# An encoder block in fp32r triples: the squares of x by rows, with ScalarE's accumulator in place of GpSimd's adds

## The chip, the cores and the metric

One core of a Trainium2 chip runs the whole program. The metric is the device time of one execution in microseconds (us), as the median of several runs. The kernel before took 2014.98 us (three runs, 2014.74 to 2017.5).

## The reference, cut to what matters

The input x has 512 rows (tokens) of 2048 columns, all float32. One transformer layer with two attention mixers is computed:

```
h    = rmsnorm(x, g_mix)                      # x * rsqrt(mean(x*x, over 2048 columns) + 1e-6) * g_mix
proj = h @ w_in                               # 2048 x 4608: qA, kA, vA, qB, kB, vB
...                                           # mixer A (grouped queries, axial rotary), mixer B (dilated windows)
x = x + concat(rmsnorm(A), rmsnorm(B)) @ w_out
x = x + (silu(h2 @ w_gate) * (h2 @ w_up)) @ w_down      # h2 = rmsnorm(x, g_ffn)
return rmsnorm(x, g_final)
```

The change is in the first line. The kernel multiplies x times the gain, without the norm, by w_in, and scales rows of the product afterwards by r = rsqrt(mean(x*x) + 1e-6). So the sum of squares of each row of x isn't needed before the first products are scaled.

## The kernel before, in words

**Products.** Every matrix product is made of three TensorE matmuls on fp32r numbers (mm3, L235 to L237): an operand is split into a rounded part "hi" and the rest "lo", and hi times hi, hi times lo and lo times hi are added up. A weight tile of 128x512 is split by a copy on ScalarE (hi; L287, or L776 in column blocks) and a subtraction on VectorE (lo; L292, or L779). So every weight that TensorE multiplies costs one 128x512 operation on each of these two engines.

**Units.** The program is a list of units, worked off in order by the loop at the end (L1309 ff.). A unit is one weight tile and its matmuls. Units 0 to 15 are the 16 chunks (128 of the 2048 columns of x) of the first projection block, keys and values of mixer A, "kvA" (first_chunk): 12 matmuls each, on all four row tiles of x. From unit 16 on stands the first "column block" (ColBlock), whose units have 6 matmuls each: it forms sums and differences of blocks, as Strassen's scheme does, and so needs sums of quarters of x (x_sums, L355) and their splits (x_split, L350 and L351), and sums of weight tiles (L816). Later come the second column block, the attention, the output projection and the feed-forward layer; they are not touched.

**What the loop does for unit n.** It issues the load of chunk n+5 of x (load_x, on SyncE's queue, SP). It prepares chunk n+1 (x_prep): four transposes on TensorE into a PSUM bank (L316), a copy of it with the gain on ScalarE (L330), hi on ScalarE (L331), lo on VectorE (L332), and row_squares, below. It then loads and splits weights some units ahead (prepare), issues the matmuls of unit n, what follows a unit (post), and what is hung on unit n (hook). For chunk pairs the hooks are, two and three units after the pair is there, x_sums (four VectorE operations of 128x256) and x_split (three operations on ScalarE, three on VectorE); and on GpSimd's queue a store of one form to DRAM (L336). Each engine works off its own instructions in the order in which the loop issued them, and starts none ahead of one that still waits.

**Squares, before.** row_squares(k) is issued within x_prep(k). ScalarE squares the chunk in place (L370; chunk 0 goes to sq1, L368), as a tile of 128 rows by 4 row tiles by 128 columns, and GpSimd adds the 128x512 squares to sq1 (L371), from chunk 1 on. The hook of unit 20 (make_r1) reduces sq1 over the columns on VectorE (L387) and makes r of it by a power on GpSimd (L217); the evictions of the column block (L864) wait for r.

**Homes.** Tiles of 128x512 numbers for loads are handed out from a list, "homes": at first 20 of the tile stage and 3 of the tile early (its fourth is sq1). A chunk of x takes one, which goes back behind its square and add; a weight takes one, which goes back when it is split, and goes to the next load in the list. The four of early leave the list at unit 12 (EARLY_HOMES; one that is in use then comes back later), and four of a tile "more" join it at unit 21. When unit 15 ends, post_plain evicts the four PSUM banks of kvA on ScalarE (L470), each into a home, from which a DMA on ScalarE's own queue stores it to DRAM (L457).

Of the kernel before, what the change touches and what calls it, by code (L numbers as in the profile page):

```python
# [11 lines left out]
F32 = mybir.dt.float32  # L12
# [44 lines left out]
HEAD_RATE = (1.42, 1.9)  # L57
TURN_LAG = 6
VALUE_LAG = 8
EARLY_HOMES = 12  # L60
COLUMN_BLOCKS = 2


# [5 lines left out]
def encoder_block(ctx, tc, x, g_mix, w_in, g_q_a, g_k_a, g_out_a, g_out_b, w_out, g_ffn,  # L69
# [40 lines left out]

    xs = [None] * KD
    stage = wp.tile([P, 20, 512], F32, tag="stage", bufs=1, name="stage")
    homes = deque(stage[:, n] for n in range(20))
    homing = [True]
    extra_homes, retired = {}, []

# [11 lines left out]
    def leave_homes():  # L128
        homing[0] = False
        homes.clear()  # L130

    def load_x(k):
        xs[k] = homes.popleft().rearrange("p (t c) -> p t c", t=NT)
        nc.sync.dma_start(xs[k], x[0, :, k * P:(k + 1) * P].rearrange("(t p) c -> p t c", p=P))

    fixed = cp.tile([P, 512], F32, name="fixed")
# [176 lines left out]
    def x_prep(k):  # L313
        ps = bank()
        for t in range(NT):
            nc.tensor.transpose(ps[:, t * P:(t + 1) * P], xs[k][:, t, :], ident)  # L316
        i, half = divmod(k, 2)
        if half == 0:
            xpair[i] = in_turn(pairs_turn, 3, [P, 4 * 512], F32, "xpair")
        flat = xpair[i][:, half * 1024:half * 1024 + 512]  # L320
        view = flat.rearrange("p (f c) -> p f c", c=256)
        hi, lo = (form_pair(3 * half, i, j) for j in range(2))
        gain = gm[:, k:k + 1]
        if k == 0:
            ps3 = ps.rearrange("p (f c) -> p f c", c=256)
            nc.scalar.activation(hi, ps3, AF.Copy, scale=gain)
            nc.vector.scalar_tensor_tensor(lo, ps3, gain, f32(hi), op0=OP.mult, op1=OP.subtract)
            nc.scalar.activation(flat, ps, AF.Copy, scale=gain)
        else:
            nc.scalar.activation(flat, ps, AF.Copy, scale=gain)  # L330
            nc.scalar.activation(hi, view, AF.Copy)  # L331
            nc.vector.tensor_tensor(lo, view, f32(hi), op=OP.subtract)  # L332
        release(ps)
        row_squares(k)
        if half == 0:
            hook(k, lambda: nc.gpsimd.dma_start(ar_dram[:, i], arena[0][:, 1, i]))  # L336
        else:
            hook(k + 2, lambda: x_sums(i))
            hook(k + 3, lambda: x_split(i))
# [18 lines left out]
        tt(s2, s1, a_l)  # L358
        tt(s4, b_l, s2)

    early = sp.tile([P, 4, 512], F32, tag="rowss", bufs=1, name="early")
    more_homes("early", early)
    sq1 = [homes.pop()]

    def row_squares(k):
        home = xs[k].rearrange("p t c -> p (t c)")
        if k == 0:
            nc.scalar.activation(sq1[0], home, AF.Square)  # L368
        else:
            nc.scalar.activation(home, home, AF.Square)  # L370
            nc.gpsimd.tensor_tensor(sq1[0], sq1[0], home, op=OP.add)  # L371
        homes.append(home)

    def col_sums(src):
        ps = bank()
# [8 lines left out]

    def make_r1():
        ss = small()
        nc.vector.tensor_reduce(ss, sq1[0].rearrange("p (t c) -> p t c", t=NT), axis=AX.X, op=OP.add)  # L387
        r1["r"] = rsqrt_mean(ss, NT, D)
        r1["rs"] = small()
        nc.vector.tensor_scalar(r1["rs"], r1["r"], HD ** -0.5, None, op0=OP.mult)  # L390
# [997 lines left out]
```

## Time and profile before

| | before |
|---|---|
| median of 3 runs | 2014.98 us |
| profiled execution, its own time | 2016.21 us |
| its span | 2014.4 us (27421 instructions) |
| granted TensorE clock, mean | 0.997 |
| TensorE (PE) busy | 1984.7 us (99%) |
| VectorE (DVE) busy | 1573.3 us (78%) |
| ScalarE (ACT) busy | 1113.9 us (55%) |
| GpSimd (POOL) busy | 154.0 us (8%) |

The profile is one execution. Times in it count from the start of the span; the execution's own time is 1.8 us longer than the span. A row of the timeline gives the start, the time, the engine, the line, the operation, the tile written and the tiles read, the shape, how many instructions alike follow each other, and in brackets how long the engine had been idle before and what ended that. A row of a group gives the busy time in us, the mean of one in ns, and the idle time in front of it. A row of the windows gives, for PE, PEld (weight loads of TensorE), DVE, ACT and POOL, busy us and the number of instructions in a stretch, then the granted clock, the share of the DMA engines and GB/s. Starts of one engine in succession lie closer than the times of single instructions, since these overlap by some 0.1 us.

### The profile page before, as it was taken

What the parts mean: (1) busy time and instruction counts of PE and PEld (TensorE: products, weight loads), DVE (VectorE), ACT (ScalarE), POOL (GpSimd) and SP (SyncE); (2) the same over time, 40 slices, a digit from 0 to 9 for tenths busy, and PEclk for the clock granted to TensorE, in tenths of its full rate; (3) what the DMA queues carried; (4) which work ended last, traced back from release to release, by engine and by line L of the source; (5) the groups of instructions that cost most, each with busy time, mean ns of one, the idle gap of its engine ahead of it and who ended that gap; (6) DMA issues with size and microseconds to landing.
All of it is one profiled execution on the core that took longest, in us unless ns stands there. A gap on an engine that the chain in (4) does not pass through costs nothing. (4 is left out here: it accounts for less than half of the span.)

```text
span 2014.4 us, 27421 instructions
## 1 busy us (share of the span) xinstructions
PE 1984.7 (99%) x9019; PEld 1630.5 (81%) x9019; DVE 1573.3 (78%) x2781; ACT 1113.9 (55%) x1972; POOL 154.0 (8%) x172
## 2 busy tenths in 40 slices
PE   8999999999999999999999999999999999999998
PEld 6788888887788888888888888888888887788886
DVE  7988866567754688878877878878779886977967
ACT  7655345556544565555555545455555665666656
POOL 4100100000010000000000000000000121111121
PEclk9999999999999999999999999999999999999999
DMA  8576533335244545737647657558468798779865
GB/s 268 188 262 223 184 116 104 110 115 184 89 137 150 200 138 201 272 120 261 239 137 273 203 182 274 170 189 285 146 215 269 194 248 257 188 175 274 207 146 165
DMA packets 231391, 390.61 MB, mean 194 GB/s; under 512 B 21408, under 2 KB 70352, under 8 KB 231120
## 3 DMA queue, kind: packets, MB, share of 16 engines
q1 hardware_dynamic: 204880, 326.13, 48.3%
q0 software_dynamic: 14960, 33.04, 8.1%
q10 hardware_dynamic: 11408, 29.70, 4.3%
q8 instruction: 70, 1.15, 0.2%
q14 instruction: 73, 0.60, 0.1%
HBM read 325.08 MB, written 63.70 MB: 193 GB/s over the span
## 5 line engine op out<-in xcount | busy, mean ns | idle before, releaser
L235 PE MATMUL b<-tw,arena 128*128 128x512 f32 x2136 | 837.6, 392 | 4.1 <-ACT ev L1154 2.2
L236 PE MATMUL b<-tw,arena 128*128 128x512 f32 x2136 | 832.8, 390 | 3.7 <-DVE tw L779 2.6
L237 PE MATMUL b<-tw,arena 128*128 128x512 f32 x2136 | 833.0, 390 | 2.8 <-DVE arena L332 2.5
L776 ACT ACTIVATE tw<-raw 128x512 fp32r<-128x512 f32 x924 | 559.3, 629 | 439.6 <-DVE raw L816 286.0
L779 DVE TENSOR_TENSOR tw<-raw,tw 128x512 fp32r<-128x512 f32 x924 | 619.2, 687 | 175.2 <-ACT tw L776 172.1
L236 PEld LDWEIGHTS b<-tw,arena 128*128 128x128 f32 x2136 | 401.2, 188 | 89.5 <-DVE tw L779 6.7
L237 PEld LDWEIGHTS b<-tw,arena 128*128 128x128 f32 x2136 | 401.0, 188 | 89.6 <-DVE arena L332 6.1
L235 PEld LDWEIGHTS b<-tw,arena 128*128 128x128 f32 x2136 | 401.1, 188 | 86.7 <-ACT ev L1154 2.9
L816 DVE TENSOR_TENSOR raw<-raw,raw 128x512 f32<-128x512 f32 x528 | 361.6, 685 | 1.0 <-DMA raw<-in_w_gate_up_dram 0.8
L1155 POOL DMA_DIRECT2D x1d<-ev x76 | 66.6, 978 | 1152.6 <-ACT ev L1154 1147.6
L235 PE MATMUL b<-w,arena 128*128 128x512 f32 x368 | 146.1, 397 | 0.0
L237 PE MATMUL b<-w,arena 128*128 128x512 f32 x368 | 143.9, 391 | 0.0
L236 PE MATMUL b<-w,arena 128*128 128x512 f32 x368 | 143.5, 390 | 0.0
L237 PEld LDWEIGHTS b<-w,arena 128*128 128x128 f32 x368 | 69.1, 188 | 15.0
L236 PEld LDWEIGHTS b<-w,arena 128*128 128x128 f32 x368 | 69.2, 188 | 14.3 <-DVE w L292 0.4
L235 PEld LDWEIGHTS b<-w,arena 128*128 128x128 f32 x368 | 69.1, 188 | 13.5
L776 ACT ACTIVATE tw<-stage 128x512 fp32r<-128x512 f32 x90 | 54.5, 629 | 42.2 <-DVE stage L816 33.8
L292 DVE TENSOR_TENSOR w<-raw,w 128x512 fp32r<-128x512 f32 x96 | 64.8, 685 | 6.3 <-ACT w L287 3.3
L227 DVE TENSOR_TENSOR pTl<-b,pTh 128x512 fp32r<-128x512 f32 x64 | 43.9, 687 | 31.7 <-ACT pTh L226 28.3
L355 DVE TENSOR_TENSOR pair<-pair 128x256 f32<-128x256 f32 x120 | 45.5, 421 | 26.4 <-ACT pair L1011 25.4
L287 ACT ACTIVATE w<-raw 128x512 fp32r<-128x512 f32 x96 | 58.2, 622 | 14.0 <-PE b L236 8.1
L1154 ACT ACTIVATE ev<-b,smalls 128x512 f32<-128x512 f32 x76 | 49.6, 683 | 26.3 <-PE b L237 25.1
(197 smaller groups left out, 1799.4 us busy)
## 6 DMA issues: line engine op xcount, KB each, us to landing
raw<-in_w_gate_up_dram SPq DMA_DIRECT2D x616, 256.0 KB, 5.3
raw<-in_w_down_dram SPq DMA_DIRECT2D x176, 256.0 KB, 7.0
stage<-in_w_in_dram SPq DMA_DIRECT2D x106, 256.0 KB, 4.9
forms<-pair SPq DMA_DIRECT2D x22, 896.0 KB, 5.3
x1d<-ev POOLq DMA_DIRECT2D x76, 256.0 KB, 6.5
fr<-forms ACTq DMA_DIRECT2D x35, 512.0 KB, 5.9
raw<-in_w_in_dram SPq DMA_DIRECT2D x64, 256.0 KB, 4.4
raw<-in_w_out_dram SPq DMA_DIRECT2D x32, 512.0 KB, 4.5
```

What stands on the lines that cost most here:

```text
L227: nc.vector.tensor_tensor(lo, src, f32(hi), op=OP.subtract)
L235: nc.tensor.matmul(dst, ah, bh, start=start, stop=False, skip_group_check=chained)
L236: nc.tensor.matmul(dst, ah, bl, start=False, stop=False, skip_group_check=chained)
L237: nc.tensor.matmul(dst, al, bh, start=False, stop=stop, skip_group_check=chained)
L287: nc.scalar.activation(self.w[0], src, AF.Copy)
L292: nc.vector.tensor_tensor(self.w[1], self.src, f32(self.w[0]), op=OP.subtract)
L355: nc.vector.tensor_tensor(out, x, y, op=op)
L776: nc.scalar.activation(self.pair[:, 0], self.src, AF.Copy)
L779: nc.vector.tensor_tensor(self.pair[:, 1], self.src, f32(self.pair[:, 0]), op=OP.subtract)
L816: nc.vector.tensor_tensor(t[dst], t[src[0]], t[src[1]], op=OP.add if form == "m6" else OP.subtract)
L1154: nc.scalar.activation(e, box.bank_of(form)[t], AF.Copy, scale=r2["r"][:, row:row + 1])
L1155: nc.gpsimd.dma_start(x1_dram[2 * cb + j, row], e, accum_op=OP.add)
```

## The change

x is kept in four "group tiles" of 128 rows by 4 row tiles by 512 columns. Four chunks of x make a group, and each chunk is loaded into its 128 columns of the group's rows. So a row tile of a group, 128x512, holds 512 columns of the same rows, and one ScalarE operation squares it and sums it over the columns (accum_out) into one column of x_ss; 16 such operations (L369) cover x. They are issued in the loop for units 3 to 18, after x_prep and ahead of prepare: group 0 in units 3 to 6, group 1 in 7 to 10, group 2 in 11 to 14, group 3 in 15 to 18. The groups lie in stage[:, :4], stage[:, 4:8], early, and stage[:, :4] again. The 15 adds on GpSimd are gone; make_r1 reduces 16 columns instead of 512. The list of homes starts with 12 tiles of stage (8 to 19); the four of group 1 join it behind unit 10's square, those of group 3 behind unit 18's, and "more" as before. EARLY_HOMES and its hook are gone. Line numbers of the changed kernel are 2 to 3 higher than before in the places named (L330 is L333, L287 is L290, L776 is L774, L470 is L468, L457 is L455).

```diff
-    homes = deque(stage[:, n] for n in range(20))
+    homes = deque(stage[:, n] for n in range(8, 20))
...
+    early = sp.tile([P, NT, 512], F32, tag="rowss", bufs=1, name="early")
+    x_groups = [stage[:, :4], stage[:, 4:8], early, stage[:, :4]]
...
     def load_x(k):
-        xs[k] = homes.popleft().rearrange("p (t c) -> p t c", t=NT)
+        lo = k % 4 * P
+        xs[k] = x_groups[k // 4][:, :, lo:lo + P]
...
         release(ps)
-        row_squares(k)
...
-    def row_squares(k):
-        home = xs[k].rearrange("p t c -> p (t c)")
-        if k == 0:
-            nc.scalar.activation(sq1[0], home, AF.Square)
-        else:
-            nc.scalar.activation(home, home, AF.Square)
-            nc.gpsimd.tensor_tensor(sq1[0], sq1[0], home, op=OP.add)
-        homes.append(home)
+    x_ss = small(4 * NT)
+
+    def row_squares(n):
+        g, t = (3, n - KD + 1) if n >= KD - 1 else divmod(n - 3, NT)
+        if 0 <= g < 4 and 0 <= t < NT:
+            row = x_groups[g][:, t]
+            nc.scalar.activation(row, row, AF.Square, accum_out=x_ss[:, 4 * t + g:4 * t + g + 1])
+            if g in (1, 3) and t == NT - 1:
+                homes.extend(x_groups[g][:, i] for i in range(NT))
...
-        nc.vector.tensor_reduce(ss, sq1[0].rearrange("p (t c) -> p t c", t=NT), axis=AX.X, op=OP.add)
+        nc.vector.tensor_reduce(ss, x_ss.rearrange("p (t c) -> p t c", t=NT), axis=AX.X, op=OP.add)
...
-    hook(EARLY_HOMES, lambda: fewer_homes("early"))
...
+        if n < KD + 3:
+            row_squares(n)
         prepare(n)
```

The order of TensorE's instructions stays as it was, and that of the loads on SP; VectorE's differs in nothing but the shape of the one reduce. What moves stands on ScalarE and on GpSimd. In the rows below a name with a number is a buffer, and "waits" names the semaphores that an instruction waits for.

On ScalarE at the very start of the program, from the gain copy of chunk 0 into xpair (L328) to the weights of units 1 to 3 (L287), the kernel before has the squares of chunks 0 and 1 between them:

```order
L328 ACTIVATE xpair_168<-b_73,fixed 128x512 [waits DVE_49]
L368 ACTIVATE early<-stage 128x512 [waits DMAHW1_49]
L330 ACTIVATE xpair_168<-b_74,fixed 128x512 [waits PE_49]
L331 ACTIVATE arena_85<-xpair_168 128x2x256 [waits Activation_49]
L370 ACTIVATE stage<-stage 128x512 [waits DMAHW3_49]
L287 ACTIVATE tw_161<-stage 128x512 [waits DMAHW5_49]
L287 ACTIVATE tw_161<-stage 128x512 [waits DMAHW7_49]
L287 ACTIVATE tw_161<-stage 128x512 [waits DMAHW1_49]
```

and the changed kernel has none until unit 3:

```order
L331 ACTIVATE xpair_168<-b_73,fixed 128x512 [waits DVE_49]
L333 ACTIVATE xpair_168<-b_74,fixed 128x512 [waits PE_49]
L334 ACTIVATE arena_86<-xpair_168 128x2x256 [waits Activation_49]
L290 ACTIVATE tw_161<-stage 128x512 [waits DMAHW5_49]
L290 ACTIVATE tw_161<-stage 128x512 [waits DMAHW7_49]
L290 ACTIVATE tw_161<-stage 128x512 [waits DMAHW1_49]
```

So the hi of chunk 1 has one square less ahead of it, and that of weight 1 two.

On ScalarE at the end of unit 15, where the four banks of kvA are evicted (L470) and stored (L457) between the weight splits of units 19 to 21, the kernel before has:

```order
L776 ACTIVATE tw_161<-stage 128x512 [waits DMAHW0_49]
L470 ACTIVATE stage<-b_75 128x512 [waits PE_49,Pool_49]
L457 DMA kvA<-stage 128x512 [waits DMAHW6_49,Activation_49]
L470 ACTIVATE stage<-b_76 128x512 [waits PE_49,Pool_49]
L457 DMA kvA<-stage 128x512 [waits DMAHW7_49,Activation_49]
L470 ACTIVATE stage<-b_77 128x512 [waits PE_49,Pool_49]
L457 DMA kvA<-stage 128x512 [waits DMAHW1_49,Activation_49]
L470 ACTIVATE stage<-b_78 128x512 [waits PE_49]
L457 DMA kvA<-stage 128x512 [waits DMAHW3_49,Activation_49]
L776 ACTIVATE tw_161<-stage 128x512
L776 ACTIVATE tw_161<-early 128x512 [waits DMAHW2_49]
```

and the changed kernel:

```order
L369 ACTIVATE stage,smalls<-stage 128x512 [waits DMAHW3_49,DMAHW6_49,DMAHW2_49,DMAHW1_49]
L774 ACTIVATE tw_161<-stage 128x512 [waits DMAHW0_49]
L468 ACTIVATE stage<-b_75 128x512 [waits PE_49]
L455 DMA kvA<-stage 128x512 [waits DMAHW2_49,Activation_49]
L468 ACTIVATE stage<-b_76 128x512 [waits PE_49]
L455 DMA kvA<-stage 128x512 [waits DMAHW3_49,Activation_49]
L468 ACTIVATE stage<-b_77 128x512 [waits PE_49]
L455 DMA kvA<-stage 128x512 [waits DMAHW4_49,Activation_49]
L468 ACTIVATE stage<-b_78 128x512 [waits DMAHW2_49,PE_49]
L455 DMA kvA<-stage 128x512 [waits DMAHW6_49,Activation_49]
L369 ACTIVATE stage,smalls<-stage 128x512
L774 ACTIVATE tw_161<-stage 128x512 [waits DMAHW1_49]
```

The evictions wait no longer for GpSimd, whose adds had last read the homes. The fourth takes the home of the first, so it waits for the first one's store (DMAHW2). Three squares stand behind the evictions that stood ahead of them before: one ahead of the split of unit 20, one ahead of that of unit 22 and one ahead of that of unit 23; and one more stands ahead of the split of unit 19.

On GpSimd, between its setup and make_r1, the kernel before had 15 adds (L371) and 8 stores (L336) in turn, of which the first are:

```order
L371 TENSOR_TENSOR early<-early,stage 128x512 [waits DMAHW3_49,Activation_49]
L336 DMA ar<-arena_84 128x512 [waits DVE_49]
L371 TENSOR_TENSOR early<-early,stage 128x512 [waits DMAHW6_49,Activation_49,Pool_49]
L371 TENSOR_TENSOR early<-early,stage 128x512 [waits DMAHW0_49,Activation_49,Pool_49]
L336 DMA ar<-arena_84 128x512 [waits DVE_49]
```

The changed kernel has from its setup to the first stores of the column block:

```order
L338 DMA ar<-arena_85 128x512 [waits DVE_49] x8
L220 ISA
L220 TENSOR_TENSOR smalls<-smalls,fixed 128x4 [waits DVE_49]
L455 DMA qA_97<-ends_743 128x512 [waits DMASW0_49,DVE_49]
L455 DMA qA_97<-ends_743 128x512 [waits DMASW1_49,DVE_49]
```

The eight stores and the power stay.

More of the change, by code (lines that the diff above doesn't have):

```diff
@@ L59 @@
 VALUE_LAG = 8
-EARLY_HOMES = 12
 COLUMN_BLOCKS = 2
@@ L359, in form_sums @@
         tt(s4, b_l, s2)
-    early = sp.tile([P, 4, 512], F32, tag="rowss", bufs=1, name="early")
-    more_homes("early", early)
-    sq1 = [homes.pop()]
-    def row_squares(k):
-        home = xs[k].rearrange("p t c -> p (t c)")
-        if k == 0:
-            nc.scalar.activation(sq1[0], home, AF.Square)
-        else:
-            nc.scalar.activation(home, home, AF.Square)
-            nc.gpsimd.tensor_tensor(sq1[0], sq1[0], home, op=OP.add)
-        homes.append(home)
+    x_ss = small(4 * NT)
[6 more added lines that the diff above has]
+                homes.extend(x_groups[g][:, i] for i in range(NT))
     def col_sums(src):
```

## The prediction

> **What bounds the kernel now.** I read the page's head first, then TensorE's waits in the stage of the first 16 units, the windows by stage, the groups by shape, and the timeline where a wait ends.
>
> ```profile
> PE 1984.7 (99%) x9019; PEld 1630.5 (81%) x9019; DVE 1573.3 (78%) x2781; ACT 1113.9 (55%) x1972; POOL 154.0 (8%) x172
> ```
>
> TensorE bounds the whole, and the change leaves its instructions alone. So the change can win only what TensorE waits in the stage that it touches, and lose only by new waits. TensorE's waits from 9 to 62 us (in total, times, longest), and two windows:
>
> ```profile
> PE b L237 <- DVE arena L332: 2.5, 5, 0.7
> PE b L236 <- DVE tw L292: 0.9, 1, 0.9
> ```
>
> ```profile
> 50.00:60.00 10.00, 9.33 (x45) 7.13 (x44) 9.93 (x16) 8.21 (x16) 6.51 (x5) 1.00 0.23 71
> 90.00:100.00 10.00, 10.00 (x46) 8.29 (x45) 9.95 (x18) 6.50 (x11) 0.00 (x0) 1.00 0.29 98
> ```
>
> From 50 to 60 us VectorE is busy for 9.93 of 10 us and TensorE for 9.33; what TensorE waits for is VectorE's lo of x (L332) and of weights (L292). From 90 us on TensorE is full, although VectorE is full too: it then runs ahead of need. How much is lost is read better from the starts of units, because a restart costs TensorE more than the wait that is listed. The transposes open a unit:
>
> ```profile
> 9.79 0.60 PE L316 MATMUL b<-fixed,stage 128*128 128x128 f32 x4
> ...
> 14.59 0.60 PE L316 MATMUL b<-fixed,stage 128*128 128x128 f32 x4
> ...
> 17.79 0.60 PE L316 MATMUL b<-fixed,stage 128*128 128x128 f32 x4
> ```
>
> ```profile
> 56.88 0.60 PE L316 MATMUL b<-fixed,stage 128*128 128x128 f32 x4
> ...
> 64.17 0.39 PE L235 MATMUL b<-tw,arena 128*128 128x512 f32 x1
> ```
>
> Unit 2 took 17.79 - 14.59 = 3.20 us and nothing waited in it. Unit 1 took 4.80, 1.6 too many. Units 2 to 13 took 56.88 - 14.59 = 42.29 us against 12 x 3.20 = 38.4; 0.45 of the 3.9 are two small transposes of gains that stay, which leaves 3.4. Units 14 and 15 took 64.17 - 56.88 = 7.29; unit 15 has no transposes and is 12 matmuls at 0.23, 2.77, so 3.20 + 2.77 = 5.97 are due and 1.3 are lost. Together **6.3 us** are lost before unit 16.
>
> **The adds that go.** Why is VectorE full? Its groups by shape, and GpSimd's:
>
> ```profile
> L355 DVE TENSOR_TENSOR pair<-pair 128x256 f32<-128x256 f32 x120 | 45.5, 421 | 26.4 <-ACT pair L1011 25.4
> ...
> L355 DVE TENSOR_TENSOR xpair<-xpair 128x256 f32<-128x256 f32 x32 | 18.3, 610 | 0.3
> L332 DVE TENSOR_TENSOR arena<-xpair,arena 128x512 fp32r<-128x512 f32 x15 | 15.7, 1049 | 7.3 <-ACT arena L331 7.3
> ```
>
> ```profile
> L371 POOL TENSOR_TENSOR early<-early,stage 128x512 f32<-128x512 f32 x14 | 23.1, 1649 | 27.4 <-ACT stage L370 18.1 <-issue 9.2
> ```
>
> The same line and shape, L355, takes 610 ns here and 421 later; L332 takes 1049 on average. The timeline shows which cases are long:
>
> ```profile
> 27.08 1.30 POOL L371 TENSOR_TENSOR early<-early,stage 128x512 f32<-128x512 f32 x1 [1.14 <-ACT stage L370]
> ```
>
> ```profile
> 27.17 1.77 DVE L332 TENSOR_TENSOR arena<-xpair,arena 128x512 fp32r<-128x512 f32 x1
> ...
> 61.02 0.68 DVE L332 TENSOR_TENSOR arena<-xpair,arena 128x512 fp32r<-128x512 f32 x1
> ```
>
> The L332 that starts just behind an add of 1.30 lasts 1.09 us longer than the one with no add beside it. Against undisturbed prices, L355 loses 32 x 0.19 = 6.0 us and L332 15 x 0.37 = 5.5, so 11.5 us over some 15 units, nearly 0.8 a unit. Undisturbed, two units ask VectorE for four 128x512 operations at 0.60 from start to start, four sums in 1.54 and three splits in 1.35: 5.3 us, 2.65 a unit, below TensorE's 3.20. With 0.8 more it is 3.4, above. So the adds make VectorE the bound of this stage, and without them TensorE should run at 3.20. That is worth the 3.4 and the 1.3.
>
> The Trainium skill, "SBUF — State Buffer", section "Who interferes with whom", says that a VectorE instruction with two SBUF inputs and a GpSimd instruction that reads SBUF exclude each other, and that whoever issues first holds the ports while the other is blocked. By it, adds that start second would cost VectorE nothing, and the sum would keep only unit 1's term. The long L332 began 0.09 us behind its add, so the trace has the case that costs VectorE.
>
> **The squares that leave the start.** Unit 1's loss isn't the adds' doing:
>
> ```profile
> 7.58 0.62 ACT L368 ACTIVATE early<-stage 128x512 f32<-128x512 f32 x1
> 8.10 0.68 ACT L330 ACTIVATE xpair<-b,fixed 128x512 f32<-128x512 f32 x1
> 8.81 0.63 ACT L331 ACTIVATE arena<-xpair 128x512 fp32r<-128x512 f32 x1
> 9.35 0.62 ACT L370 ACTIVATE stage<-stage 128x512 f32<-128x512 f32 x1
> ```
>
> Two squares at 0.52 from start to start stand ahead of the hi of weight 1, which ends at 10.4; its lo on VectorE is the 0.9 us of waiting for L292. Without them hi ends at 9.4 and lo at 10.2, before TensorE's first product of unit 1 at 10.5. That is the **1.6 us**.
>
> **What the new squares cost ScalarE.** The final norm has a square with accumulator of the same size:
>
> ```profile
> 1977.29 0.63 ACT L1199 ACTIVATE jf<-x 128x512 f32<-128x512 f32 x1 [0.62 <-DVE x L1202]
> 1977.83 0.18 ACT L1199 ACTIVATION_READ_ACCUMULATOR jf<-x 128x1 f32 x1
> 1977.92 1.28 ACT L776 ACTIVATE tw<-raw 128x512 fp32r<-128x512 f32 x2
> ```
>
> It holds the engine for 0.63 us to the next instruction, where a plain square holds it for 0.52. Two units then ask ScalarE for 2 x (0.72 + 0.54 for x, 0.63, 0.52 for a weight) and 1.14 of x_split, 5.96 us against TensorE's 6.40. It fits, with 0.2 a unit to spare; that is the cover.
>
> **Where it gives some back: from unit 15 to unit 25.** In before:
>
> ```profile
> 62.34 0.60 ACT L470 ACTIVATE stage<-b 128x512 f32<-128x512 f32 x1
> 62.98 0.35 ACTq L457 DMA_DIRECT2D kvA<-stage  x1
> ...
> 66.50 0.63 ACT L776 ACTIVATE tw<-stage 128x512 fp32r<-128x512 f32 x1 [0.40 <-ACT stage L470]
> ```
>
> ```profile
> DMA to landing us min/median/max: 2.2/2.6/3.0
> ```
>
> The four evictions with their stores take 66.50 - 62.34 = 4.16, 1.04 each, and the hi of unit 20 follows at once. Unit 20 begins four units of 1.36 behind 64.17, at 69.61, so ScalarE is 3.1 us ahead there. Afterwards unit 16 begins at 64.17 - 6.3 = 57.87 and unit 20 at 63.31. ScalarE begins unit 14's work at 52.5, when its transposes are done; two x copies, two squares, three weights, x_split are 5.2 us, so the first eviction starts at 57.73. The fourth waits for the first store: issued at 58.37, landed 2.6 later, at 61.0. With its own store it is done at 62.0, one square more is 62.63, and unit 20's hi only starts there: 0.7 ahead instead of 3.1. VectorE's order makes it worse, since the lo of units 21 and 22 stand behind x_split and x_sums:
>
> ```profile
> 68.00 1.52 DVE L351 TENSOR_TENSOR arena<-xpair,arena 128x256 fp32r<-128x256 f32 x3
> 69.43 0.68 DVE L779 TENSOR_TENSOR tw<-early,tw 128x512 fp32r<-128x512 f32 x1
> 70.04 1.55 DVE L355 TENSOR_TENSOR xpair<-xpair 128x256 f32<-128x256 f32 x4
> ```
>
> Unit 20's lo is then ready 0.5 late; ScalarE's x_split ends at 64.8, so unit 21's lo ends at 66.0, another 1.0 late with the restart; unit 22's, behind 1.55 of sums, 0.65; unit 23's, behind one more square, 0.5. That is 2.7 us, where before lost 0.9 in units 23 and 25 (0.3 and 0.6). The cost is **1.8 us**. Its ends are 0, if ScalarE is done earlier than I reckon, and 4.3, if the store lands as late as the loads below (5.2).
>
> **Edits at nothing.** The reduce of 16 columns, and make_r1's instructions otherwise unchanged, are off TensorE's path. x's loads move the same bytes in the same order. The load of chunk 12 now waits for unit 6's square, at some 28 us; its transposes come at 42 or later.
>
> One home fewer from unit 21 on (24 against 25) lets each load wait for the next split, 1.2 us later. In before:
>
> ```profile
> 103.67 2.01 SPq L264 DMA_DIRECT2D stage<-in_w_in_dram  x4
> ```
>
> ```profile
> 113.12 0.68 DVE L816 TENSOR_TENSOR stage<-stage 128x512 f32<-128x512 f32 x1
> ```
>
> ```profile
> stage<-in_w_in_dram SPq DMA_DIRECT2D x16, 256.0 KB, 5.2
> ```
>
> The load issued at 103.67 is used at 113.12, 9.4 us later, and 8.2 later afterwards; it lands in 5.2 (the median from 104 to 118 us). I take nothing.
>
> **The sum.** 1.6 + 3.4 + 1.3 - 1.8 = 4.5 us less. The profiled execution's own time is 2016.21, which becomes 2011.7; the median of the runs is 1.23 lower, 2014.98, and becomes **2010.5**. From some unit 32 on everything should merely stand 4.5 us earlier.
>
> **Rivals.**
>
> - *The transition costs nothing more.* ScalarE's new work falls into its idle times at units 21 to 25, or the first store lands before the fourth eviction is due. Then all 6.3 stay: 2008.7; and 2007.8 if the old 0.9 goes too. For it: each of the reckoned stalls is 1.0 us or less, which the working by hand can miss. Against: 3.1 us of lead shrink to 0.7.
> - *The fourth eviction waits longer.* Should the first store land 5.2 us after its issue, in a queue full of loads, the transition costs 4.3 and 2.0 is left: 2013.0. Against: the four stores took 2.2 to 3.0 in before; but more loads may be under way beside them.
> - *VectorE isn't freed.* If its long operations have another cause than the adds, unit 1's 1.6 and the 1.8 cancel: 2015.2. Against it stand the pairs of rows above.
> - *Slower: one home fewer starves the first column block.* Were a load to take more than the 8.2 us that are left, every round of the homes would be late by the rest. Some 88 loads over 24 homes are 3.7 rounds, and the lead of some 4 us over TensorE covers the first of it. At 12 us a load, (12 - 8.2) x 3.7 - 4 = 10 us are lost behind a gain of 4.5: 2020.5. It decides from 11.5 us a load on. The median is 5.2, so little speaks for it.
>
> **How the numbers follow.** A measurement tells 0.2%, 4 us, from no change. The forecast has 0.52, with its terms good for about a microsecond: 2009.3 to 2011.7, most of it below 2011.0, the line for faster. The free transition has 0.20, the longer wait 0.15, VectorE not freed 0.05, starved loads 0.08. Faster: 0.20 and 0.40 of the forecast's 0.52, 0.60. Same: 0.12 + 0.15 + 0.05 = 0.32. Slower: 0.08. The range takes in the first three cases with their bounds and the third's edge, 2007.2 to 2015.2.
>
> **What would show it.** In the profile after, L335 (now lo of x) should take 0.68 us throughout and VectorE be idle at times from 20 to 60 us; unit 2's transposes should start near 13.0, unit 14's near 51.9, unit 16 near 57.9; the fourth L468 should start near 61.0; TensorE's waits from 63 to 72 us should sum to some 2.7 for L774 and L777. If unit 14 isn't near 52, the reason given for VectorE is wrong; if unit 16 is right and the time isn't, the transition or the loads behind it are.

## The result, and the profile after

The changed kernel takes 2011.61 us (median of 22 runs, 2009.15 to 2014.04), before 2014.96 (22 runs, 2013.61 to 2017.5): 3.35 us less, a ratio of 0.9983 with a 95% interval of 0.9977 to 0.9989. The profiled execution took 2011.22 us.

The page's head, and the window that the prediction showed:

```profile
span 2009.4 us, 27417 instructions
...
PE 1984.8 (99%) x9019; PEld 1632.0 (81%) x9019; DVE 1562.4 (78%) x2781; ACT 1114.6 (55%) x1988; POOL 127.4 (6%) x157
```

```profile
50.00:60.00 10.00, 10.00 (x48) 8.25 (x47) 8.98 (x19) 8.69 (x20) 0.54 (x1) 1.00 0.16 53
90.00:100.00 10.00, 10.00 (x46) 8.27 (x45) 9.68 (x17) 5.95 (x11) 0.00 (x0) 1.00 0.01 2
```

From 50 to 60 us TensorE is full, where it had 9.33, and VectorE, with the adds gone, has a tenth of its time left. The groups of VectorE say why:

```profile
L357 DVE TENSOR_TENSOR xpair<-xpair 128x256 f32<-128x256 f32 x32 | 12.1, 420 | 0.3
L335 DVE TENSOR_TENSOR arena<-xpair,arena 128x512 fp32r<-128x512 f32 x15 | 10.4, 692 | 11.0 <-ACT arena L334 10.4
```

The sums of x take 420 ns instead of 610 and the lo of x 692 instead of 1049: both are what the same operations take elsewhere. TensorE's starts of units 1, 2, 14 and 16:

```profile
9.35 0.60 PE L319 MATMUL b<-fixed,stage 128*128 128x128 f32 x4
...
12.86 0.60 PE L319 MATMUL b<-fixed,stage 128*128 128x128 f32 x4
...
51.69 0.60 PE L319 MATMUL b<-fixed,stage 128*128 128x128 f32 x4
...
57.62 0.39 PE L238 MATMUL b<-tw,arena 128*128 128x512 f32 x1
```

Units 2 to 13 take 38.83 us (42.29 before), units 14 and 15 5.93 (7.29): nothing is lost there. Then comes what is given back. ScalarE at the end of unit 15:

```profile
57.51 0.58 ACT L468 ACTIVATE stage<-b 128x512 f32<-128x512 f32 x1
...
60.59 0.60 ACT L468 ACTIVATE stage<-b 128x512 f32<-128x512 f32 x1 [0.46 <-PE b L240]
...
62.25 1.14 ACT L774 ACTIVATE tw<-stage 128x512 fp32r<-128x512 f32 x2
```

The first eviction starts at 57.51, the fourth at 60.59, and the hi of unit 20 at 62.25, 0.8 us ahead of unit 20 (63.07). TensorE's waits behind it:

```profile
63.64 0.50 PE L239 MATMUL b<-tw,arena 128*128 128x512 f32 x1 [0.17 <-DVE tw L777]
65.90 0.50 PE L239 MATMUL b<-tw,arena 128*128 128x512 f32 x1 [0.60 <-DVE tw L777]
67.96 0.50 PE L239 MATMUL b<-tw,arena 128*128 128x512 f32 x1 [0.39 <-DVE tw L777]
69.84 0.50 PE L239 MATMUL b<-tw,arena 128*128 128x512 f32 x1 [0.21 <-DVE tw L777]
```

One wait in each of units 20 to 23. So far the prediction holds to a few tenths. But TensorE has other waits far behind the change. Its waits in the attention, in the kernel before between the products at 459.86 and 513.25 us:

```profile
PE b L582 <- DVE pTl L227: 2.5, 1, 2.5
PE b L235 <- DVE pTl L227: 0.3, 1, 0.3
```

and in the changed kernel between the same products, at 454.12 and 510.18:

```profile
PE b L580 <- DVE pTl L230: 2.4, 1, 2.4
PE b L238 <- DVE pTl L230: 1.3, 2, 0.7
PE b L239 <- DVE w L295: 0.7, 1, 0.7
PE b L238 <- ACT acc L603: 0.5, 1, 0.5
```

Three more waits, in a stretch where the change edits nothing and TensorE's order is the same. The stretch takes 56.1 us instead of 53.4. One step ahead of it stands ScalarE, first in before, then in the changed kernel:

```profile
458.31 0.60 ACT L226 ACTIVATE pTh<-b 128x512 fp32r<-128x512 f32 x1 [1.05 <-PE b L582]
```

```profile
453.85 0.60 ACT L229 ACTIVATE pTh<-b 128x512 fp32r<-128x512 f32 x1 [2.27 <-DMA oA<-oT]
```

The same operation, which writes a tile of attention weights (pTh), waits for its input in before, and in the changed kernel for a store of another tile, oT, to have landed (issued at 449.39, landed at 453.77). No data passes between these two. But in the changed program this pTh has been laid at the address in SBUF where that oT lay just before it (220288 in each partition); in before it lies at 148608, away from it. So the wait comes from where tiles lie. The experiments test whether the other waits do too.

### The profile page after: what moved, and what is told of

It is laid out like the page before. It is cut to its first block, busy times and chain, and to the rows that moved or that the text cites. A ratio compares the mean times of both kernels' runs of the same rounds, so it can differ in the third digit from the quotient of the medians.

```text
span 2009.4 us, 27417 instructions
## 1 busy us (share of the span) xinstructions
PE 1984.8 (99%) x9019; PEld 1632.0 (81%) x9019; DVE 1562.4 (78%) x2781; ACT 1114.6 (55%) x1988; POOL 127.4 (6%) x157
## 5 line engine op out<-in xcount | busy, mean ns | idle before, releaser
L774 ACT ACTIVATE tw<-raw 128x512 fp32r<-128x512 f32 x924 | 558.6, 628 | 436.6 <-DVE raw L814 285.9
L240 PEld LDWEIGHTS b<-w,arena 128*128 128x128 f32 x368 | 69.1, 188 | 14.9
L774 ACT ACTIVATE tw<-stage 128x512 fp32r<-128x512 f32 x93 | 55.6, 627 | 41.0 <-DVE stage L814 30.6
L777 DVE TENSOR_TENSOR tw<-stage,tw 128x512 fp32r<-128x512 f32 x93 | 61.5, 684 | 13.6 <-ACT tw L774 13.6
L295 DVE TENSOR_TENSOR w<-raw,w 128x512 fp32r<-128x512 f32 x96 | 64.7, 684 | 6.0 <-ACT w L290 3.5
L290 ACT ACTIVATE w<-raw 128x512 fp32r<-128x512 f32 x96 | 58.3, 623 | 15.5 <-PE b L239 6.9
L357 DVE TENSOR_TENSOR pair<-pair 128x256 f32<-128x256 f32 x120 | 45.5, 420 | 26.2 <-ACT pair L1009 25.1
```

Source lines behind the costliest of these rows:

```text
L240: nc.tensor.matmul(dst, al, bh, start=False, stop=stop, skip_group_check=chained)
L290: nc.scalar.activation(self.w[0], src, AF.Copy)
L295: nc.vector.tensor_tensor(self.w[1], self.src, f32(self.w[0]), op=OP.subtract)
L357: nc.vector.tensor_tensor(out, x, y, op=op)
L774: nc.scalar.activation(self.pair[:, 0], self.src, AF.Copy)
L777: nc.vector.tensor_tensor(self.pair[:, 1], self.src, f32(self.pair[:, 0]), op=OP.subtract)
```

## The experiments

One table carries most readings. It gives when the same instruction of TensorE starts in every kernel's profile (TensorE's order is the same in all), and the times between. The marks are the transposes of unit 2, the first product of unit 16, the last product ahead of unit 26 (78.50 in before; called unit 26 below), the transpose just ahead of the first product with w (459.83 in before; called w), and a product in the output projection (513.25 in before). "Clock" is when the granted clock first became full.

| kernel | clock | unit 2 | 2 to 16 | 16 to 26 | 26 to w | w to 513 | median of runs, ratio to before, interval |
|---|---|---|---|---|---|---|---|
| before | 4.0 | 14.59 | 49.58 | 14.33 | 381.33 | 53.42 | 2014.96 |
| before_again | 4.5 | 14.50 | 49.60 | 14.37 | 381.45 | 53.51 | 2014.81, one run |
| changed | 4.5 | 12.86 | 44.77 | 16.07 | 380.40 | 56.08 | 2011.61, 0.9983 (0.9977 to 0.9989) |
| after_again | 4.8 | 12.86 | 44.76 | 16.12 | 380.48 | 55.92 | 2012.2, 0.9987 (0.9978 to 0.9996) |
| adds_back | 9.7 | 14.48 | 46.91 | 15.18 | 380.46 | 58.34 | 2011.88, 0.9989 (0.9981 to 0.9997) |
| adds_double | 4.4 | 12.80 | 57.68 | 14.32 | 380.49 | 55.93 | 2024.09, 1.0047 (1.0033 to 1.006) |
| no_adds | 6.3 | 14.14 | 44.77 | 15.24 | 381.25 | 53.39 | 2010.81, 0.9982 (0.9973 to 0.9991) |
| late_first | 5.5 | 13.19 | 51.95 | 14.33 | 381.60 | 53.45 | 2016.75, 1.0008 (1.0 to 1.0017) |
| squares_late | 9.0 | 14.19 | 44.76 | 14.77 | 380.45 | 55.13 | 2007.65, 0.9963 (0.9951 to 0.9975) |
| pool_early_late | 8.6 | 14.02 | 44.76 | 13.37 | 380.45 | 55.88 | 2007.19, 0.9961 (0.9949 to 0.9974) |
| before_places | 5.9 | 13.20 | 44.77 | 16.07 | 381.21 | 53.44 | 2010.65, 0.9975 (0.9964 to 0.9986) |
| late_places | 9.7 | 14.93 | 44.76 | 14.76 | 381.53 | 53.42 | 2009.49, 0.9974 (0.9964 to 0.9984) |
| pel_places | 4.1 | 12.87 | 44.76 | 13.37 | 381.05 | 53.51 | 2009.62, 0.9969 (0.9959 to 0.998) |
| no_more | 4.1 | 12.76 | 44.76 | 16.07 | 381.51 | 53.54 | 2008.67, 0.9972 (0.996 to 0.9984) |

In the two kernels that were profiled twice these stages repeat to 0.2 us, while single runs of one kernel spread over 4 us. So the stages decide about causes, and the medians only about a few microseconds. Not every stage repeats so well: after_again names one far behind that does not.

### no_adds: before without GpSimd's adds

```diff
         else:
             nc.scalar.activation(home, home, AF.Square)
-            nc.gpsimd.tensor_tensor(sq1[0], sq1[0], home, op=OP.add)
```

> The kernel before without its 15 adds on GpSimd, so that the norm is made from the squares of the first chunk alone; all else stays, the squares too. Theory V: 3.4 + 1.3 of the 6.3 us that are lost before unit 16 go and the 1.6 of unit 1 stay, so unit 16 starts near 59.5 instead of 64.2; of this about 1 us is given back behind it, and the time is some 4 us below before's 2015.0. Rival S: unit 16 stays at 64 and the time is that of before.

This kernel leaves the sum over the chunks out, so that its norm is made from the first chunk alone. Unit 2 to unit 16 takes 44.77 us, 4.81 less than in before and the same as in the changed kernel. The lo of x takes what it takes there:

```profile
L332 DVE TENSOR_TENSOR arena<-xpair,arena 128x512 fp32r<-128x512 f32 x15 | 10.4, 693 | 11.9 <-ACT arena L331 11.9
```

Theory V holds, and rival S falls: the squares stood where they had stood. Unit 16 starts at 58.90 instead of the 59.5 that I expected, since unit 2 is earlier by 0.45 too, with both squares in place. The lo of weights 1 and 2, first in before (beside an add from 10.05 to 11.33), then here:

```profile
10.52 1.95 DVE L292 TENSOR_TENSOR tw<-stage,tw 128x512 fp32r<-128x512 f32 x2 [0.35 <-ACT tw L287]
```

```profile
10.79 1.29 DVE L292 TENSOR_TENSOR tw<-stage,tw 128x512 fp32r<-128x512 f32 x2 [0.35 <-ACT tw L287]
```

The first add held these two up by 0.66 us, so unit 1's loss was in part an add's doing. The time, 2010.81, is 3.95 below before's on the same chip (2014.76).

### adds_back and adds_double: one add, then two, behind each of 12 squares

```diff
             nc.scalar.activation(row, row, AF.Square, accum_out=x_ss[:, 4 * t + g:4 * t + g + 1])
+            if n < KD - 1:
+                nc.gpsimd.tensor_tensor(row, row, row, op=OP.add)
```

adds_double has this last line in a loop of two.

> The changed kernel with a GpSimd add put back behind each of the first 12 squares (units 3 to 14): the squared row is doubled in place, which reads and writes as much as the adds of before and changes no number that the output needs. Theory V (an add of GpSimd holds VectorE off, and so VectorE becomes the bound of units 3 to 15): the lo of x takes over 1.5 us in many units again, TensorE waits for it, unit 16 starts 3 to 4.5 us later than in the changed kernel (57.8 us), near 61.5, and the time is some 3 us above the changed kernel's 2011.6. Rival S (the gain comes from where the squares stand on ScalarE, and adds only filled GpSimd): unit 16 stays within 0.5 us of 57.8 and the time within 1 us of 2011.6.

> The changed kernel with two GpSimd adds behind each of the first 12 squares, in place of one in adds_back; they double the squared row, whose numbers nothing needs any more. Theory V: an add costs VectorE 0.8 us wherever it stands, so 12 more adds cost some 9.6 us of VectorE, none of which lies in spare time any more, since one add a unit had used that up (adds_back lost 2.1 us between unit 2 and unit 16). Unit 2 to unit 16 takes 44.8 us in the changed kernel, 46.9 in adds_back and should take 54 to 57 here; time 8 to 11 us above the changed kernel's. Rival (GpSimd is held by VectorE at least as much, so its second add waits for gaps that VectorE leaves): under 50 us.

With one add, L335 takes 966 ns on average and L295 999, where the changed kernel has 692 and 684; with 442 for L357 that makes 9.8 us, 0.8 an add. Unit 16 starts at 61.39, about where I expected it, but 1.6 us of its delay stand ahead of unit 2, where the clock became full late. Only 2.1 us of the adds' cost reach TensorE (46.91 against 44.77), less than the 3 to 4.5 that I expected, and 0.9 of that is won back up to unit 26 (15.18 against 16.07). The times of the runs don't tell the two kernels apart. The adds begin at unit 3, so there are 12 and not 15; and VectorE may have been further ahead, as unit 2 began later, which wasn't tried by itself. The profile is that of the slowest of the 12 runs (2019.64), with four dips of the clock, all behind unit 26. With two adds, what was left of VectorE's time is used up:

```profile
PE b L240 <- DVE arena L335: 9.4, 6, 3.7
```

```profile
L372 POOL TENSOR_TENSOR stage<-stage 128x512 f32<-128x512 f32 x16 | 21.3, 1334 | 13.7 <-ACT stage L369 13.0
```

Unit 2 to unit 16 takes 57.68, 12.9 more than without adds, and the kernel 2024.09, 9.5 above before. 24 adds at 0.8 are 19 us of VectorE; VectorE's own 2.65 us a unit leave 0.55 of room, 6.6 in 12 units, so some 12.6 are due. The rival's 50 is far away. The same sum gives 3.0 for 12 adds, where 2.1 were measured, so it is good to about a microsecond. (In this profile the clock dips to half from 55.6 to 59.0 us, which may have a part in the 12.9, by 3.4 us at half clock at most 1.7.) GpSimd's add takes 1.33 us here against 1.65 in before; it is VectorE that is held.

The rows also show how one add does it. In adds_double 24 operations of VectorE are long, 20.0 us in all beyond their usual times; in adds_back 12 are, 10.1 in all: one operation for each add, by 0.84 us on average. In before 13 are long, 13.4 in all, with 15 adds (1.03 each; these adds read two tiles, the ones put back read one row twice). This holds for adds that start second too, first VectorE and then GpSimd in before:

```profile
49.01 0.68 DVE L332 TENSOR_TENSOR arena<-xpair,arena 128x512 fp32r<-128x512 f32 x1
49.61 0.68 DVE L292 TENSOR_TENSOR tw<-stage,tw 128x512 fp32r<-128x512 f32 x1
50.22 2.52 DVE L355 TENSOR_TENSOR xpair<-xpair 128x256 f32<-128x256 f32 x4
```

```profile
49.18 3.27 POOL L371 TENSOR_TENSOR early<-early,stage 128x512 f32<-128x512 f32 x1 [2.34 <-ACT stage L370]
```

The add begins 0.17 us behind the lo of x, which keeps its usual 0.68, and lasts 3.27; the four sums further on take 2.52 instead of 1.54. So an add that starts second waits, and then holds up a later operation. Only the two adds at 13.43 and 17.24 hold up none: behind the operation that each of them waits for, VectorE is idle for 1.9 to 2.5 us.

### late_first: two squares and adds out of units 0 and 1

```diff
         release(ps)
-        row_squares(k)
+        if k > 1:
+            row_squares(k)
...
-        if k == 0:
+        if k == 2:
             nc.scalar.activation(sq1[0], home, AF.Square)
...
+        if n in (3, 5):
+            row_squares(n // 4)
         prepare(n)
```

> The kernel before with only the squares and adds of chunks 0 and 1 moved, from units 0 and 1 to units 3 and 5. My theory of unit 1 (two squares on ScalarE stand ahead of the hi of weight 1): unit 2's transposes start at 13.0 instead of 14.6, the 0.9 us of waiting for L292 is gone. What becomes of the 1.6 us later: if VectorE is the bound of units 3 to 15, its two displaced adds hold it there too, and unit 16 starts 1 to 1.6 us earlier than 64.2; time 2013.4 to 2014.2. Rival: the first weights' loads are late, and unit 2 stays at 14.6.

Unit 2 starts at 13.19 and the wait for L292 is gone, as expected for units 0 and 1 without squares and add. The rest of the expectation failed: unit 16 starts 1 us later than in before, not 1 to 1.6 earlier, and the time, 2016.75, is no better (the interval of its ratio begins at 1.0).

```profile
PE b L237 <- DVE arena L332: 4.7, 6, 1.3
```

The worst place is the sums of x in unit 4, GpSimd first and VectorE behind it:

```profile
19.05 4.70 POOL L372 TENSOR_TENSOR early<-early,stage 128x512 f32<-128x512 f32 x3 [1.47 <-ACT stage L371]
```

```profile
19.63 4.86 DVE L356 TENSOR_TENSOR xpair<-xpair 128x256 f32<-128x256 f32 x4
```

TensorE waits for the lo of x for 4.7 us instead of 2.5. The displaced add comes between two others, so that three run in a row, and the four sums, 1.54 without adds, take 4.86: 3.3 more, 1.1 an add, which is what the others cost too. What I had overlooked is that before's first three adds are nearly free: they hold VectorE up by 0.67 us in all, since it is idle behind two of them. Here all 15 hold up one operation each, 16.2 us in all against 13.4 in before, and all of them from unit 2 on.

### squares_late and pool_early_late: the transition at unit 16

squares_late:

```diff
-        g, t = (3, n - KD + 1) if n >= KD - 1 else divmod(n - 3, NT)
+        g, t = (3, n - KD - 3) if n >= KD - 1 else divmod(n - 3, NT)
...
-    hook(20, make_r1)
+    hook(22, make_r1)
...
-        if n < KD + 3:
+        if n < KD + 7:
             row_squares(n)
```

and pool_early_late beside it:

```diff
-            e = homes.popleft() if name == "kvA" else slot("ev" + name)
+            e = early[:, t] if name == "kvA" else slot("ev" + name)
...
-            store(name, t, e, nc.scalar)
-            if name == "kvA":
-                homes.append(e)
+            store(name, t, e, nc.gpsimd if name == "kvA" else nc.scalar)
```

> The changed kernel with the four squares of group 3 issued four units later (units 19 to 22, which puts them behind the weight splits of units 20 to 23), and make_r1 at unit 22 instead of 20. Theory T (the 1.8 us given back from unit 20 to 25 are ScalarE's squares and evictions in front of the splits): the hi of unit 20 starts 0.8 to 1.2 us earlier against unit 16's start, the waits of units 20 to 23 fall from 2.0 us of lost time to 0.3 to 0.8, and the time is some 1.3 us below the changed kernel's. Rival: VectorE's order (x_split and x_sums ahead of the lo of units 21 and 22) sets these waits, and they stay within 0.4 us of what they are.

> The changed kernel with group 3's squares four units later, the four kvA rows evicted into the tile early, which is free by then, and their stores issued on GpSimd's queue instead of ScalarE's. Theory T: ScalarE saves 0.4 us a store and the wait for the first store, so unit 20's hi starts 1 to 1.6 us earlier still against unit 16's start, and what squares_late still loses between units 20 and 25 (0.4 us) goes; 0.3 to 0.5 us below squares_late up to unit 26. Rival (GpSimd's issues hold VectorE off, as its adds did): VectorE's operations near the stores take over 0.2 us longer and units 20 to 23 lose 0.5 us or more.

Unit 16 to unit 26 takes 14.77 in squares_late, 1.3 less than in the changed kernel; two waits of 0.6 in all are left of four. ScalarE there, the fourth eviction and the hi of units 20 and 21:

```profile
61.32 0.60 ACT L468 ACTIVATE stage<-b 128x512 f32<-128x512 f32 x1 [0.46 <-DMA kvA<-stage]
...
62.35 1.15 ACT L774 ACTIVATE tw<-stage 128x512 fp32r<-128x512 f32 x2 [0.43 <-ACT stage L468]
```

Here the first store is named as what the fourth eviction waits for, but the 0.46 us is no longer than the gap in the changed kernel, and most of it is the issue of the third store (0.33 us). In pool_early_late neither this wait nor the issue of stores is on ScalarE:

```profile
58.08 2.03 ACT L468 ACTIVATE early<-b 128x512 f32<-128x512 f32 x4
59.99 1.16 ACT L772 ACTIVATE tw<-stage 128x512 fp32r<-128x512 f32 x2
```

Four evictions take 2.03 us instead of 4.1, unit 20's hi starts 4.2 us ahead of unit 20, and unit 16 to unit 26 takes 13.37: no wait is left. Theory T holds, and GpSimd's issues hold nobody up: the four sums of x beside them, from 58.90, take 1.55 us, as in squares_late. I expected 0.3 to 0.5 us of it beyond squares_late; it is 1.4, since squares_late still lost more than the listed waits say. That is the lowest median of all, 2007.19, a ratio of 0.9961 (0.9949 to 0.9974); the runs don't tell it from squares_late.

Up to unit 26 squares_late is 1.3 us better than the changed kernel, by its runs 3.96 (2007.65 against 2011.61). 0.8 to 0.9 of the rest stand between w and 513, where its profile has no dip of the clock; pool_early_late, whose tiles lie at the same places, has one there and takes 55.88. Another 1.5 stand between the marks at 1705.07 and 1738.54 us in before, which take 31.97 us in squares_late and 32.13 in pool_early_late where before takes 33.47. These two share an arrangement of tiles of their own; that it is the cause of the 1.5 is not shown.

### after_again and before_again: what of the profiles repeats

Neither has an edit.

> The changed kernel once more, for a second profile. Its first one gained 4.8 us up to unit 26 and 0.9 more up to 460 us, and lost 2.7 between 460 and 512 us, where it waits for a w (L295), for acc (L603) and for pTl (L230) as before doesn't. Theory P (these waits are built in, since the change lets tiles of the attention lie elsewhere in SBUF): the same waits come again, and the stretch that runs from 459.8 to 513.3 us in before takes 54.4 to 55.2 us besides 1.7 for each dip of the granted clock in it, where before takes 51.7 besides. Rival N (that profile was an outlier): 51.7 to 52.3 besides dips.

> The kernel before once more, for a second profile. The stretch of 53.4 us from 460 to 512 us and the 381.3 from unit 26 on should come again to within 0.3 us; the 14.75 us that the first profile shows between 1690 and 1705 us, where the other kernels with the same places take 11.7 to 12.3, should not. If the granted clock becomes full later than at 4.0 us, unit 2 should still start at 14.6 or little later, since two squares on ScalarE hold it there and not TensorE.

Both repeat. 56.08 and 55.92 us in the changed kernel, 53.42 and 53.51 in before: the three waits of the attention are built in. (The 1.7 us that I put down for each dip was wrong, as before_places shows.) What didn't repeat is in the first profile of before: 14.75 us between 1690.32 and 1705.07, which take 11.39 in its second profile and 11.85 and 12.80 in the two of the changed kernel (11.3 to 15.5 in all 14 profiles). So 2.9 of the 5.0 us between the first two spans (2014.4 and 2009.4) are chance there, and a dip of the clock at 1728 us in the changed kernel takes 1.6 back. Unit 2 starts at 14.50 as expected, but the clock was full at 4.5 us, so what a late clock does to before wasn't seen.

### before_places, late_places and pel_places: where tiles lie

```diff
-    hook(21, lambda: more_homes("more", wp.tile([P, 4, 512], F32, tag="more", bufs=1, name="more")))
+    def more():
+        tile = wp.tile([P, 4, 512], F32, tag="more", bufs=1, name="more")
+        more_homes("more", tile)
+        hook(118, lambda: nc.gpsimd.memset(tile[:, 0, :1], 0.0))
+    hook(21, more)
+    hook(109, lambda: nc.gpsimd.memset(early[:, 0, :1], 0.0))
```

The packer that lays tiles into SBUF goes by how long each is in use. In before, early is in use up to unit 109, since one of its homes came back into the list; in the changed kernel it is free after unit 14, and more is free earlier too. So 50 of the 64 tiles of pTh and 695 of 856 tiles of raw weights lie at other addresses than in before. The two memsets keep both tiles in use. In before_places 10 of the 64 and 111 of the 856 still lie elsewhere; in late_places (the edits of squares_late beside them) and pel_places (those of pool_early_late) no tile does.

> The changed kernel with two GpSimd memsets of one column, in early at unit 109 and in more at unit 118, that write nothing that is read again: they keep these two tiles occupied about as long as in before, and so nearly all tiles of the attention lie where they lay in before. Theory P: the waits for acc, w and pTl between 452 and 512 us go, the stretch takes 51.7 us besides dips of the clock, the 0.9 won between unit 26 and 460 us go too (381.3 instead of 380.4), and the time is 1 to 2 us below the changed kernel's, 4 to 5 below before's. Rival M (the stage in front runs 5 us earlier and so its loads collide differently with the attention's): both stretches and the time stay those of the changed kernel.

> The changed kernel with the squares of group 3 four units later and with the two memsets, which give every tile the place that it had in before. Theory T and theory P together: 1.2 us less than before_places up to unit 26, and 51.7 us besides dips in the stretch from 460 to 512; time 5.5 to 6.5 us below before's. Rival M: the stretch stays at 54.4 to 55.2, and the time is that of squares_late on the same chip.

> pool_early_late with the two memsets that give every tile the place that it had in before. Theories T and P: units up to 26 as in pool_early_late, the stretch from 460 to 512 us 53.4 instead of 55.9, unit 26 to 460 us 381.2 instead of 380.5, and the 1.5 us that pool_early_late and squares_late win between 1705 and 1740 us, where their tiles lie elsewhere too, given up: within 1 us of pool_early_late, 7 to 8 us below before.

All three take 53.4 to 53.5 us between w and 513, and 381.05 to 381.53 from unit 26 to w. TensorE's waits of before_places in that stretch:

```profile
PE b L585 <- DVE pTl L230: 2.5, 1, 2.5
PE b L238 <- DVE pTl L230: 1.9, 2, 1.5
```

The waits for w and acc are gone. Theory P holds, and rival M falls, since the stage in front still runs 4 to 8 us earlier. Two other kernels say the same from the other side. adds_double, whose tiles all lie as in the changed kernel, reaches w 5.5 us later than before does and still takes 55.93; no_adds, whose tiles all lie as in before, reaches it 4.4 us earlier and takes 53.39. The 0.9 us up to w goes by the places too: 380.4 to 380.5 in the six profiles of changed, after_again, adds_back, adds_double, squares_late and pool_early_late, 381.05 to 381.6 in the seven with all or most tiles at the old places. I expected 51.7 besides dips of the clock; it is 53.4 with and without a dip. before has one at 485.2 us, before_places none, and there TensorE waits 1.5 for pTl in its place. So with the old places the dip costs nothing there: the waits behind VectorE's pTl take up its time.

The medians go the same way, though not exactly: before_places is 1 us below the changed kernel, late_places 5.3 below before (5.5 to 6.5 expected). pel_places, 2009.62, should have been within 1 us of pool_early_late and is 2.4 above it; the intervals of the two overlap, and its profile takes 32.77 between the marks at 1705 and 1738, 0.6 more than pool_early_late's. What made up the rest in those runs is open.

### no_more: four homes fewer

```diff
-    hook(21, lambda: more_homes("more", wp.tile([P, 4, 512], F32, tag="more", bufs=1, name="more")))
...
-    last.after("m5", 0, lambda: fewer_homes("more"))
```

> The changed kernel without the tile more, so that 20 homes carry the loads of the first two column blocks instead of 24. It tests the price of a home that the prediction used for its slower rival: each home fewer lets a load wait 1.2 us longer, so that of the 8.2 us between issue and use some 3.4 are left, against 5.2 until landing. By that price each round of the homes is 1.8 late, some 4.4 rounds make 8, and the lead of 4 us covers the first half: unit 26 to 460 us takes some 4 us longer than 380.4, time 3 to 5 us above the changed kernel's. Rival (loads are issued early enough, and homes aren't what they wait for): within 1 us.

The rival's reason is right, though neither time came out as said: homes aren't what the loads wait for. From unit 26 to w it takes 381.51, 1.1 more than the changed kernel instead of 4, and within 0.5 of the kernels with the old places. TensorE has no wait for a load; VectorE waits 1.6 us in all for loads, in four sums of weights. And since more isn't there, the tiles of the attention lie in a third arrangement, which takes 53.54 from w to 513. So up to 513 leaving the tile out wins 1.5 us on the changed kernel; by the medians it is 2.9 (2008.67), with intervals that overlap. My price of a home was wrong by its whole size.

## Why the prediction was right, and where it was not

The time came out in the range, on the side that was forecast, and 1.1 us above the forecast (2011.61 against 2010.5). It is 0.6 above 2011.0, the line below which the prediction spoke of faster, so its likeliest outcome, at 0.60, did not come. The range reached up to no change at all, so that a time within it says little for the mechanism; the starts of units say more. By the prediction's steps:

- **Unit 1's squares, 1.6 us.** Unit 2 starts 1.73 us earlier with the clock full at 4.5 us, and 1.64 between the two repeated profiles. late_first gives 1.40. But not all of it is the squares': no_adds has them and starts unit 2 0.45 earlier, and the lo of weight 1 was held up by the first add as well. "Unit 1's loss isn't the adds' doing" was wrong by about that much. With the clock full only at 8.6 to 9.7 us, kernels with the new order start unit 2 at 14.0 to 14.9; no profile of before fell there, so what the term is worth in such runs is open.
- **The adds on VectorE, 3.4 + 1.3.** Measured 42.29 - 38.83 = 3.46 and 7.29 - 5.93 = 1.36. no_adds shows that the adds are the cause, and adds_double how the cost grows. The Trainium skill's rule ("SBUF — State Buffer", "Who interferes with whom") agrees in that two inputs from SBUF and a GpSimd instruction exclude each other; but what the prediction drew from it, that adds which start second would cost VectorE nothing, came out for two of before's 15 adds alone. The others hold up one operation each, those that start second a later one. The 11.5 us of the prediction left out what two splits of weights lost (L292, 0.67 and 1.10 us).
- **The transition, -1.8.** 16.07 against 14.33: 1.74. Against pool_early_late's 13.37, where nothing waits, the changed kernel loses 2.70 and before 0.96; 2.7 and 0.9 were worked out. TensorE's listed waits sum to 1.4 and not to the 2.7 that the prediction looked for, since it took lost time for listed waits. ScalarE's times were 0.2 to 0.4 earlier than worked out. The wait for the first store cost little in the changed kernel (60.59, where TensorE's last bank is named as the one waited for), more of it the three squares, 1.30 as squares_late shows.
- **The step that failed: "From some unit 32 on everything should merely stand 4.5 us earlier."** At unit 26 it stood 4.8 earlier, at w 5.7 (5.7 also between the repeated profiles), and at 513 only 3.1 (3.3). The waits of the attention took 2.4 to 2.7 back, and 0.9 was won ahead of it. The prediction looked at the order of instructions and at the homes, and left out that a tile's time in use sets where later tiles lie, and so what they wait for. The 3.1 to 3.3 us that are left at 513 are near what the medians show, 3.35, though further on two profiles of before differ by 3.4 in one stretch alone.
- **One home fewer, nothing.** Right in the sum, wrong in its price, as no_more shows; so the slower rival was no rival at all.

Of the other rivals, a free transition and a longer wait for the store didn't come; VectorE was freed.

## What to carry to other kernels

Look for one shape at two durations, as 421 and 610 ns here: an operation on an engine with time to spare may hold a neighbour off, and it costs about what exceeds the neighbour's room, and nothing where the neighbour would have been idle. Where a packer lays tiles, a change of a tile's time in use can move waits hundreds of microseconds behind it, so compare the waits of the whole kernel, and try another arrangement before a far wait is explained by the edit. Where runs spread over 4 us, compare the starts of the same instructions in two profiles, and take a second profile of the same kernel to see which stages repeat.

## What the runs showed of the hardware

The clock at the start is a matter of chance: the granted clock became full between 4.0 and 9.7 us in 14 profiles of programs that begin with the same matmuls, and the later dips to half, but for the one at the very end, last 3.413 us each. The Trainium skill, "TensorE: Matmul & The Clock Gate", "Part 1: The HAM clock gate (the "warmup" mystery)", says that the clock is released after a busy window of about 3.4 us, that these windows run freely, and that the start therefore varies from run to run. The 3.413 us and a start that varies agree; by how much it varies does not, as the page gives 0.5 us either way and these profiles differ by 5.7. Here the first matmuls have pauses, of 0.40 and 0.93 us in before's profile, which may be why. What a dip costs depends on where it falls: nothing between w and 513 in before, 1.6 us at 1728 in the changed kernel (35.07 us between the marks at 1705 and 1738, 33.51 in after_again). Between w and 513 with the new places it is some 0.8 (55.13 without a dip in squares_late, 55.88 with one in pool_early_late), and adds_back, with two, takes 58.34.

ScalarE's square with accumulator held the engine for 0.52 us and its accumulator read for 0.09 more (56.38, 56.90 and 56.99 in the changed kernel), 0.61 in all where I had taken 0.63.
